# Groups of background products queued behind chosen products of the input GEMM, and GEMM products put between the pieces of the burst at the RWKV samples (one layer of an HGRN2 + RWKV-7 decoder)

## The chip, the cores and the metric

One core of one Trainium2 chip. The metric is the device time of one execution in microseconds (us), the median of several runs. The engines are TensorE (PE, with its weight loads PEld), VectorE (DVE), ScalarE (ACT), GpSimd (POOL) and SyncE (SP), which issues most transfers.

## What is computed

The reference is one inference step of one layer for a prompt of 512 tokens and 8 samples of 4 tokens, D_MODEL 1024, all in f32:

```python
h = RMSNorm(x)
u = h @ W_in          # 46 blocks of 128 columns: HGRN2 q,f,i,g | RWKV-7 r,k,v,lora | gates
# HGRN2 branch: 4 heads, state 128x128
S_t = diag(f_t) S_{t-1} + k_t v_t^T ;  o_t = S_t^T q_t
# RWKV-7 branch: 8 heads, state 64x64
S = S * w_t - (S kk_t)(kk_t a_t)^T + v_t k_t^T ;  y_t = S r_t
x = x + merge(sigmoid gates, projections of both branches)
x = x + relu(RMSNorm(x) @ W_up)^2 @ W_down
```

The outputs are y for prompt and samples, and both branches' new states.

## The kernel before

**The input GEMM.** Each block of 128 columns of W_in is one unit (`in_unit`, L411): its weights are loaded (`load8`, L175, 512 KB), split into a high and a low part (`split`, L167: ACT writes `whi`, DVE writes `wlo`), and `gemm_h` (L399) multiplies them with the normalised rows, kept as `h_hi` and `h_lo`. A unit is two halves of 272 columns, each 24 products: eight `h_hi,whi`, eight `h_hi,wlo`, eight `h_lo,whi`. All products pass through `mm` (L129). The results leave PSUM through ACT and DVE (`xq`, `xk`, `gt`, ...).

**The background.** The two branches run beside these GEMM products. The eight RWKV heads are four pairs p = 0 to 3 in two groups g = 0, 1. For a pair, `rw_batch` (L548) normalises k (`halves`, L534, splits the squares into `sxh` on ACT and `sxl` on POOL; `head_sums`, L540, sums them over a head on PE by two products with `sxh` and two with `sxl`; then a reciprocal `nrm` on DVE), makes `kkn`, `b`, `eb`, `kr`, sums `rk` in the same way into `bv`, and multiplies `kr` with `eb` (`rw_batch_pa`), which DVE masks into `A`. From `A`, by way of DRAM (`zb_d`), DVE inverts small blocks (`rw_inverse`, L669: `tmp`, `bn`, `xi`); then follow `rw_solve` and the chain over chunks. `rw_values` (L634) and `rw_tokens` (L647) make transposes and products with `VU`, `pav` and `BE`. `rw_sample` (L867) does the samples: for each pair 16 + 2 small products into `rw_sample_pz`, and then four rounds of eight small products, `rw_sample_pu`, each of which needs a DVE result (`rs` or `un`) made from the round before; the first round needs `rs` made from `pz` (`tsc(u0, zs, mneg, ...)`). `hg_head` (L1069) does an HGRN2 head: DVE and ACT make a decayed `X`, PE multiplies it (`hg_head_pu`, once for widths of 32 and once for 64), and its end transposes `hy` (`hg_head_pt`, L1160).

**What sets the order.** `ORDER` (L51) is a list by hand of units and of background stages; generators ("lanes") are advanced between units. What they emit is then put in order for each engine by a scheduler with its own estimates of durations; an engine executes its own instructions strictly in that order.

Of the kernel before, what the change touches and what calls it, by code (L numbers as in the profile page):

```python
# [61 lines left out]
def hybrid_step(ctx: ExitStack, tc: tile.TileContext, i, o):  # L62
# [1006 lines left out]
    def hg_head(L, h):  # L1069
# [34 lines left out]
        for hw, po_ in ((32, p32), (64, p64)):  # L1104
# [4 lines left out]
            for c in range(4):
                for u in range(64 // hw):  # L1110
                    s0 = 128 * c + 2 * hw * u
                    mm(po_[2 * hw * u:2 * hw * u + hw, c, :], X[:, s0:s0 + hw], X[:, s0 + hw:s0 + 2 * hw])
# [636 lines left out]
```

## Time and profile before

| | us |
|---|---|
| runs | 969.31, 972.62, 973.67; median 972.62 |
| profiled execution | 974.22 (span 972.5, mean granted clock 0.992) |
| PE busy | 933.1 (96% of the span) |
| DVE, ACT, POOL busy | 671.2, 444.4, 150.0 |

The profile is of one execution: start and duration of each instruction, and what an engine waited for when it was idle. A share of busy time over the whole span hides stages: the input GEMM with its background takes the part up to about 500 us, the MLP the rest. The change bears on the part from about 107 to 360 us. [...]

### The profile page before, as it was taken

The numbers are of one execution on the slowest core, as the hardware profiler recorded it, in microseconds if no ns is written. First come the engines' busy times: TensorE is split into PE (matmuls) and PEld (weight loads), VectorE is DVE, ScalarE is ACT, GpSimd is POOL, SyncE is SP. The second block draws the span as 40 slices with busy tenths as digits, with TensorE's granted clock in tenths as the row PEclk, the third lists the DMA queues.
The fourth block names the chain that finished last, engine by engine and source line by source line (L and its number), as shares of the span: only waits on it lengthen the run. The fifth ranks groups of instructions, "written<-read, shape, count | busy, mean of one in ns | idle before, by whom it ended". The sixth has DMA issues, their size and how long they took to land.

```text
span 972.5 us, 21434 instructions
## 1 busy us (share of the span) xinstructions
PE 933.1 (96%) x8756; PEld 880.5 (91%) x8756; DVE 671.2 (69%) x1362; ACT 444.4 (46%) x802; POOL 150.0 (15%) x340
## 2 busy tenths in 40 slices
PE   5999999899999899999999999999999999999995
PEld 5989987779899787888899999999999999999995
DVE  6634978769796864689878656675567667976433
ACT  7554546414636641344344334455444345435332
POOL 3487333222232101011000000000000000000000
PEclk9999999999999899999999999999999999999998
DMA  9633333312535142375734643246335533554111
GB/s 268 171 120 88 80 85 87 81 36 85 155 97 124 35 117 63 83 211 156 248 109 157 181 133 86 76 109 161 114 87 128 142 101 88 136 147 142 54 44 49
DMA packets 193204, 112.67 MB, mean 116 GB/s; under 512 B 39521, under 2 KB 179623, under 8 KB 193106
## 3 DMA queue, kind: packets, MB, share of 16 engines
q1 hardware_dynamic: 165808, 95.16, 33.7%
q10 hardware_dynamic: 25570, 9.85, 4.0%
q0 software_dynamic: 1728, 6.29, 3.4%
q8 instruction: 69, 1.13, 0.5%
q14 instruction: 29, 0.24, 0.1%
HBM read 85.08 MB, written 18.39 MB: 106 GB/s over the span
## 4 chain that ended last, share of the span: by engine, by line
PE 79%; DVE 10%; ACT 3%; DMA 3%; issue 2%; POOL 2%; SPq 0%; ACTq 0%; DVEq 0%; POOLq 0%
PE pd L130 25%; PE in_unit_ps L130 21%; PE full_unit_ps L130 17%; PE half_unit_ps L130 4%; PE rw_chain_pq L130 2%; PE rw_chain_py L130 1%; DVE tmp L136 1%; DVE wlo L136 1%; PE lora_ps L130 1%; PE rw_sample_pn L130 1%; PE hg_head_po L130 1%; PE rw_batch_pa L130 1%; DMA xin<-in_x_prompt_dram 1%; DVE X L136 1%; DMA zb_d<-A 1%
## 5 line engine op out<-in xcount | busy, mean ns | idle before, releaser
L133 ACT ACTIVATE whi<-st 128x1024 fp32r<-128x1024 f32 (+1 forms) x132 | 134.1, 1018 | 161.8 <-PE pd L130 65.6
L136 DVE TENSOR_TENSOR wlo<-st,whi 128x1024 fp32r<-128x1024 f32 (+1 forms) x120 | 142.6, 1190 | 34.1 <-ACT whi L133 11.2
L130 PE MATMUL in_unit_ps<-h_hi,whi 128*128 128x272 f32 (+3 forms) x736 | 119.6, 297 | 1.9 <-ACT h_hi L133 1.0
L130 PE MATMUL in_unit_ps<-h_hi,wlo 128*128 128x272 f32 (+3 forms) x736 | 119.6, 296 | 0.0
L130 PE MATMUL in_unit_ps<-h_lo,whi 128*128 128x272 f32 (+3 forms) x736 | 118.5, 295 | 0.0
L130 PEld LDWEIGHTS in_unit_ps<-h_hi,whi 128*128 128x128 f32 x736 | 101.6, 191 | 7.5 <-issue 3.4
L130 PE MATMUL full_unit_ps<-hd,whi 128*128 128x272 f32 (+2 forms) x736 | 108.3, 288 | 0.0
L130 PEld LDWEIGHTS in_unit_ps<-h_hi,wlo 128*128 128x128 f32 x736 | 101.7, 190 | 4.4 <-issue 2.3
L130 PEld LDWEIGHTS in_unit_ps<-h_lo,whi 128*128 128x128 f32 x736 | 101.2, 189 | 3.7 <-issue 1.9
L130 PEld LDWEIGHTS full_unit_ps<-hd,whi 128*128 128x128 f32 x736 | 98.6, 188 | 0.0
L130 PE MATMUL pd<-xgh,wlo 128*128 128x272 f32 x512 | 70.0, 288 | 0.0
L130 PE MATMUL pd<-xgl,whi 128*128 128x272 f32 x512 | 69.9, 288 | 0.0
L130 PE MATMUL pd<-xgh,whi 128*128 128x272 f32 x512 | 69.9, 288 | 0.0
L130 PEld LDWEIGHTS pd<-xgl,whi 128*128 128x128 f32 x512 | 66.5, 188 | 0.0
L130 PEld LDWEIGHTS pd<-xgh,wlo 128*128 128x128 f32 x512 | 66.5, 188 | 0.0
L130 PEld LDWEIGHTS pd<-xgh,whi 128*128 128x128 f32 x512 | 66.4, 188 | 0.0
L1602 POOL DMA_DIRECT2D slo<-st x12 | 10.5, 874 | 353.0 <-ACT slo L133 180.8
L136 DVE TENSOR_TENSOR x<-x,full_unit_ps 128x272 f32<-128x272 f32 (+3 forms) x40 | 20.8, 521 | 49.6 <-PE full_unit_ps L130 49.5
L130 PE MATMUL full_unit_ps<-hd,wlo 128*128 128x272 f32 (+2 forms) x272 | 47.7, 291 | 0.0
L130 PEld LDWEIGHTS full_unit_ps<-hd,wlo 128*128 128x128 f32 x272 | 38.8, 188 | 1.0
L133 ACT ACTIVATE gt<-in_unit_ps 128x272 f32<-128x272 f32 x32 | 12.6, 395 | 53.3 <-PE in_unit_ps L130 51.4
L139 DVE SCALAR_TENSOR_TENSOR r<-pd,rsb 128x272 f32<-128x272 f32 x64 | 25.1, 434 | 16.3 <-PE pd L130 14.3
(438 smaller groups left out, 1682.2 us busy)
## 6 DMA issues: line engine op xcount, KB each, us to landing
st<-in_w_in_dram SPq DMA_DIRECT2D x46, 512.0 KB
st<-in_w_up_dram SPq DMA_DIRECT2D x32, 512.0 KB
st<-in_w_down_dram SPq DMA_DIRECT2D x48, 256.0 KB
slo<-st POOLq DMA_DIRECT2D x12, 512.0 KB, 4.5
gt_d<-gt SPq DMA_DIRECT2D x16, 272.0 KB
st<-in_w_out_dram SPq DMA_DIRECT2D x8, 512.0 KB
st<-in_w_down_dram SPq DMA_DIRECT2D x8, 512.0 KB
gtb<-gt_d SPq DMA_DIRECT2D x8, 272.0 KB
```

The costliest lines, as they stand in the source:

```text
L130: T.matmul(out, lhsT, rhs, start=start, stop=stop)
L133: A.activation(out=out, in_=in_, func=func, **kw)
L136: (eng or V).tensor_tensor(out=out, in0=a, in1=b, op=op)
L139: V.scalar_tensor_tensor(out=out, in0=a, scalar=s, in1=b, op0=op0, op1=op1)
L1602: P.dma_start(out=w2.lo, in_=t2, accum_op=ALU.add)
```

## The change

`mm` returns its instruction; `gemm_h` counts each GEMM product in `gemms`. Inside `behind(n)`, every PE instruction that is issued gets an ordering dependency on GEMM product n: the scheduler may not place it earlier in PE's queue than that product. There is no semaphore, and no instruction of the arithmetic is added or removed. The constants give n for: the `sxl` products of `head_sums` of `bv` (PL_RK, per pair), the 32-wide `hg_head_pu` products of heads 0 and 1 (PL_PU), the `hy` transposes of head 1 (PL_HY), transposes of `eb` (PL_EB), the `pav` products of pairs 2, 3 (PL_AV), the `pz` products of pairs 1 to 3 (PL_PZ) and the first `pu` round (PL_SU).

```diff
+PL_RK = 612, 737, 1366, 1478
+PL_PU = {0: 946, 1: 1184}
+PL_HY = {1: 1280}
+PL_EB = {(0, 1): 848, (2, 0): 1560, (2, 1): 1560, (3, 0): 1568, (3, 1): 1568}
+PL_AV = {2: 1560, 3: 1568}
+PL_PZ = {1: 1576, 2: 1576, 3: 1584}
+PL_SU = {0: 1618}
...
     def mm(out, lhsT, rhs, start=True, stop=True):
-        T.matmul(out, lhsT, rhs, start=start, stop=stop)
+        return T.matmul(out, lhsT, rhs, start=start, stop=stop)
+    def queue(x, g):
+        tc.add_manual_dep(x, g.name, mybir.DependencyInfo(mybir.DependencyClass.NoSync, mybir.DependencyReason.DATA),
+                          reason="place")
+    @contextmanager
+    def behind(n):
+        cur = nc.cur_bb.bb.instructions
+        last = cur[-1]
+        yield
...
+        for x in cur[k + 1:]:
+            if x.engine == gemms[0].engine:
+                if n < len(gemms):
+                    queue(x, gemms[n])
+                else:
+                    places.setdefault(n, []).append(x)
...
-                    mm(ps, w[k], x[k][:, a:b], s == 0 and k == 0, s == 2 and k == K - 1)
+                    placed(mm(ps, w[k], x[k][:, a:b], s == 0 and k == 0, s == 2 and k == K - 1))
...
-    def head_sums(hi, lo):
+    def head_sums(hi, lo, n=None):
...
+            with behind(n) if k and n else nullcontext():
+                for j in range(2):
+                    mm(ps[:, j], bones, y[:, j * HALF:(j + 1) * HALF], k == 0, k == 1)
...
+            with behind(PL_SU[it]) if it in PL_SU else nullcontext():
```

The scheduler places everything else anew around these, so the queues of DVE, ACT, POOL and SP change too. Three places are shown (before first, the change second; line numbers of the two files differ).

The first: DVE's queue between `hy` of head 1 and the reciprocal of pair 2 (`nrm_3574`), with which the RWKV work of group 1 starts on DVE:

```order
L136 TENSOR_TENSOR hy_3472<-hy_3472,ss_h 128x512
L139 SCALAR_TENSOR_TENSOR hog_3499<-hg_head_pt_3494,prm,xq_2421 128x512
L142 TENSOR_SCALAR nrm_3574<-nrm_3574 128x544
L567 RECIPROCAL nrm_3574<-nrm_3574 128x544
L139 SCALAR_TENSOR_TENSOR xq_3663<-xq_3663,in_unit_ps_3613 128x272
L139 SCALAR_TENSOR_TENSOR kkn_3598<-xm_3229,prm,nrm_3574 128x544
```

```order
L172 TENSOR_TENSOR hy_3472<-hy_3472,ss_h 128x512
L175 SCALAR_TENSOR_TENSOR xq_3663<-xq_3663,in_unit_ps_3613 128x272
L175 SCALAR_TENSOR_TENSOR hog_3499<-hg_head_pt_3494,prm,xq_2421 128x512
L172 TENSOR_TENSOR wlo_3815<-st_3812,whi_3814 128x1024
L178 TENSOR_SCALAR nrm_3574<-nrm_3574 128x544
L604 RECIPROCAL nrm_3574<-nrm_3574 128x544
L175 SCALAR_TENSOR_TENSOR xq_3663<-xq_3663,in_unit_ps_3638 128x272
```

A GEMM result (`xq_3663`) and a weight split (`wlo_3815`) now stand ahead of the reciprocal. In POOL's queue a little later, the copy `ga<-xq_3758`, which stood behind pair 2's `sxl_3685`, now stands ahead of it.

The second: DVE's queue at the last mask of pair 3 (`A` from `rw_batch_pa_4018`), from which the inverse starts:

```order
L876 SCALAR_TENSOR_TENSOR rs_4138<-rst_351,gs 128x128
L136 TENSOR_TENSOR wlo_4545<-st_4542,whi_4544 128x1024
L136 TENSOR_TENSOR rs_4138<-rs_4138,gs 128x128
L136 TENSOR_TENSOR rs_4139<-gs,rs_4138 128x4x32
L136 TENSOR_TENSOR A_3989<-rw_batch_pa_4018,msk 128x256
L136 TENSOR_TENSOR A_3991<-rw_batch_pa_4018,msk 128x256
L136 TENSOR_TENSOR A_3990<-rw_batch_pa_4018,msk 128x256
L136 TENSOR_TENSOR A_3992<-rw_batch_pa_4018,msk 128x256
L136 TENSOR_TENSOR rs_4139<-gs,rs_4138 128x4x32 x3
```

```order
L915 SCALAR_TENSOR_TENSOR rs_4138<-rst_351,gs 128x128
L172 TENSOR_TENSOR rs_4138<-rs_4138,gs 128x128
L172 TENSOR_TENSOR rs_4139<-gs,rs_4138 128x4x32 x2
L172 TENSOR_TENSOR A_3989<-rw_batch_pa_4018,msk 128x256
L172 TENSOR_TENSOR A_3991<-rw_batch_pa_4018,msk 128x256
L172 TENSOR_TENSOR A_3990<-rw_batch_pa_4018,msk 128x256
L172 TENSOR_TENSOR A_3992<-rw_batch_pa_4018,msk 128x256
```

The four `A` now stand behind two `rs_4139<-gs,rs_4138`, the samples' keys times a decay from ACT, where before they stood behind one.

The third: the first rounds of the samples, on PE and on DVE. PE's queue at the first `pu` round; `in_unit_ps` are GEMM products, `rw_sample_pz` the end of the burst, `rw_sample_pu_4476` the first round and `rw_sample_pu_4492` the second:

```order
L130 MATMUL rw_sample_pz_4291<-s0T_4041,km_4365 64x64 x15
L130 MATMUL rw_sample_pz_4291<-rs_4141,rs_4140 64x64 x2
L130 MATMUL in_unit_ps_4548<-h_lo,whi_4544 128x272 x8
L130 MATMUL in_unit_ps_4573<-h_hi,whi_4544 128x272 x8
L130 MATMUL in_unit_ps_4573<-h_hi,wlo_4545 128x272 x8
L130 MATMUL in_unit_ps_4573<-h_lo,whi_4544 128x272 x8
L130 MATMUL in_unit_ps_4735<-h_hi,whi_4731 128x272 x4
L130 MATMUL rw_sample_pu_4476<-rs_4142,rs_4140 64x64 x8
L130 MATMUL in_unit_ps_4735<-h_hi,whi_4731 128x272 x4
L130 MATMUL in_unit_ps_4735<-h_hi,wlo_4732 128x272 x6
L130 MATMUL rw_sample_pu_4492<-rs_4142,rs_4140 64x64 x8
```

```order
L137 MATMUL rw_sample_pz_4291<-s0T_4041,km_4365 64x64 x16
L137 MATMUL rw_sample_pz_4291<-rs_4141,rs_4140 64x64 x2
L137 MATMUL in_unit_ps_4735<-h_hi,whi_4731 128x272 x7
L137 MATMUL in_unit_ps_4735<-h_hi,wlo_4732 128x272 x8
L137 MATMUL in_unit_ps_4735<-h_lo,whi_4731 128x272 x8
L137 MATMUL in_unit_ps_4760<-h_hi,whi_4731 128x272 x8
L137 MATMUL in_unit_ps_4760<-h_hi,wlo_4732 128x272 x3
L137 MATMUL rw_sample_pu_4476<-rs_4142,rs_4140 64x64 x8
L137 MATMUL in_unit_ps_4760<-h_hi,wlo_4732 128x272 x5
L137 MATMUL in_unit_ps_4760<-h_lo,whi_4731 128x272
L137 MATMUL rw_sample_pu_4492<-rs_4142,rs_4140 64x64 x8
```

The first round now stands 31 GEMM products further back: before, four of block 4735's first half lie ahead of it, now all 24 of that half (one of them ahead of the last `pz` piece) and 11 of the second half (4760). Between the first and the second round stood 10 products; now 6.

DVE's queue at the first `rs` of the samples (`rs_4142<-rs_4141`, what the first `pu` round waits for) and the second (`rs_4142<-rw_sample_pu_4476`, what the second round waits for):

```order
L136 TENSOR_TENSOR tmp_4060<-xi_4051,x_4052 128x512
L725 TENSOR_REDUCE bn_4050<-tmp_4060 128x32
L136 TENSOR_TENSOR tmp_4060<-bn_4050,x_4052 128x512
L142 TENSOR_SCALAR rs_4142<-rs_4141,mneg 128x256
L725 TENSOR_REDUCE bn_4050<-tmp_4060 128x8x8
L136 TENSOR_TENSOR tmp_4060<-bn_4050,x_4052 128x512
L139 SCALAR_TENSOR_TENSOR rs_4142<-rw_sample_pu_4476,mneg,rs_4142 128x256
L725 TENSOR_REDUCE bn_4050<-tmp_4060 128x4x8
```

```order
L175 SCALAR_TENSOR_TENSOR xq_4598<-xq_4598,in_unit_ps_4548 128x272
L172 TENSOR_TENSOR tmp_4060<-bn_4050,x_4052 128x512
L175 SCALAR_TENSOR_TENSOR xq_4598<-xq_4598,in_unit_ps_4573 128x272
L764 TENSOR_REDUCE bn_4050<-tmp_4060 128x8x8
L178 TENSOR_SCALAR rs_4142<-rs_4141,mneg 128x256
L172 TENSOR_TENSOR tmp_4060<-bn_4050,x_4052 128x512
L172 TENSOR_TENSOR s0T_4041<-s0T_4041,rs_4138 128x512
L764 TENSOR_REDUCE bn_4050<-tmp_4060 128x4x8
L172 TENSOR_TENSOR tmp_4060<-bn_4050,x_4052 128x512
L764 TENSOR_REDUCE bn_4050<-tmp_4060 128x4x8
L175 SCALAR_TENSOR_TENSOR rs_4142<-rw_sample_pu_4476,mneg,rs_4142 128x256
```

Two `xq` and one more `bn` stand ahead of the first `rs` now, and some rows earlier a seventh weight split (`wlo_4922`), where between `hy` and this `rs` stood six; one `s0T` (`s0T_4041`) has gone behind it. Between the first and the second `rs` stand two `tmp`, one `s0T` and two `bn`, where before stood one `tmp` and one `bn`.

## Rows read from the trace of the kernel before

**Rows 1.** The page, its first part: busy time, share of the span and instructions of each engine.

```profile
PE 933.1 (96%) x8756; PEld 880.5 (91%) x8756; DVE 671.2 (69%) x1362; ACT 444.4 (46%) x802; POOL 150.0 (15%) x340
```

**Rows 2.** The waits of PE from 100 to 345 us: who waits, for whom; us in total, times, the longest.

```profile
PE hg_head_pu L130 <- DVE X L136: 3.0, 1, 3.0
PE head_sums_ps L130 <- POOL sxl L136: 2.7, 4, 0.7
PE rw_sample_pu L130 <- DVE rs L142: 2.4, 1, 2.4
PE rw_batch_pt L662 <- ACT av L133: 1.6, 1, 1.6
PE hg_head_pt L1160 <- DVE hy L136: 1.4, 1, 1.4
```

**Rows 3.** Windows, busy us (and instructions) of PE, PEld, DVE, ACT, POOL, then the granted clock, the DMA share and GB/s.

```profile
160.00:180.00 20.00, 17.02 (x195) 15.33 (x194) 18.56 (x30) 8.95 (x16) 11.32 (x16) 1.00 0.46 125
...
200.00:240.00 40.00, 40.00 (x579) 33.91 (x578) 32.69 (x90) 11.34 (x20) 8.20 (x19) 1.00 0.23 70
...
260.00:280.00 20.00, 17.56 (x136) 16.77 (x135) 18.87 (x33) 10.41 (x15) 7.53 (x12) 1.00 0.45 122
...
320.00:340.00 20.00, 17.28 (x205) 15.55 (x205) 16.71 (x24) 11.54 (x18) 2.79 (x6) 0.83 0.19 40
```

**Rows 4.** The timeline of PE at the head sums of pairs 0 and 1, each with the idle time before it and its releaser in brackets.

```profile
109.01 0.52 PE L130 MATMUL head_sums_ps<-sxl,bones 128*128 128x272 f32 x2 [0.69 <-POOL sxl L136]
...
130.25 0.52 PE L130 MATMUL head_sums_ps<-sxl,bones 128*128 128x272 f32 x2 [0.73 <-POOL sxl L136]
```

**Rows 5.** The timeline of PE around the burst, from its first small products to the last `pu` round.

```profile
314.12 1.15 PE L130 MATMUL rw_sample_pz<-s0T,km 64*64 64x64 f32 x32
...
325.05 1.27 PE L130 MATMUL in_unit_ps<-h_lo,whi 128*128 128x272 f32 x8
...
329.16 0.67 PE L130 MATMUL in_unit_ps<-h_hi,whi 128*128 128x272 f32 x4
332.24 1.12 PE L130 MATMUL rw_sample_pu<-rs,rs 64*64 64x64 f32 x16 [2.41 <-DVE rs L142]
...
334.36 1.56 PE L130 MATMUL in_unit_ps<-h_hi,wlo 128*128 128x272 f32 x6
335.85 1.12 PE L130 MATMUL rw_sample_pu<-rs,rs 64*64 64x64 f32 x16
...
341.02 0.68 PE L130 MATMUL rw_sample_pu<-rs,rs 64*64 64x64 f32 x16
...
342.63 1.16 PE L130 MATMUL in_unit_ps<-h_lo,whi 128*128 128x272 f32 x8
343.63 1.17 PE L130 MATMUL in_unit_ps<-h_hi,whi 128*128 128x272 f32 x8
```

**Rows 6.** Windows of 2 us over the same stretch, columns as in group 3.

```profile
330.00:332.00 2.00, 0.00 (x0) 0.00 (x0) 1.93 (x4) 1.99 (x5) 0.37 (x2) 0.93 0.00 0
...
334.00:336.00 2.00, 2.00 (x11) 1.75 (x12) 2.00 (x4) 0.00 (x0) 0.00 (x0) 0.50 0.00 0
...
338.00:340.00 2.00, 2.00 (x26) 1.79 (x25) 0.44 (x2) 0.40 (x1) 0.46 (x2) 0.86 0.17 24
```

**Rows 7.** The timeline of DVE from `hy` of head 1 to `bv` of pair 2 and at pairs 2 and 3.

```profile
258.45 1.23 DVE L136 TENSOR_TENSOR wlo<-st,whi 128x1024 fp32r<-128x1024 f32 x1
...
262.74 0.69 DVE L136 TENSOR_TENSOR hy<-hy,ss_h 128x512 f32<-128x512 f32 x1
...
265.32 3.55 DVE L567 RECIPROCAL nrm<-nrm 128x544 f32<-128x544 f32 x1
268.79 0.38 DVE L139 SCALAR_TENSOR_TENSOR xq<-xq,in_unit_ps 128x272 f32<-128x272 f32 x1
...
277.25 2.37 DVE L136 TENSOR_TENSOR wlo<-st,whi 128x1024 fp32r<-128x1024 f32 x1
...
304.01 1.42 DVE L136 TENSOR_TENSOR A<-rw_batch_pa,msk 128x256 f32<-128x256 f32 x4
307.09 0.69 DVE L136 TENSOR_TENSOR rs<-gs,rs 128x128 f32<-128x128 f32 x3 [1.66 <-ACT rs L133]
```

**Rows 8.** The timeline of POOL in the same stretch.

```profile
258.63 2.28 POOL L136 TENSOR_TENSOR sxl<-sq,sxh 128x544 fp32r<-128x544 f32 x1 [3.19 <-ACT sxh L133]
...
277.05 1.49 POOL L136 TENSOR_TENSOR sxl<-rk,sxh 128x544 fp32r<-128x544 f32 x1 [2.41 <-ACT sxh L133]
278.48 1.21 POOL L1039 COPY ga<-xq 128x32 f32<-128x32 f32 x1
```

**Rows 9.** The timeline of DVE in the inverse of group 1, up to the `rs` of the first and the second `pu` round.

```profile
320.58 1.22 DVE L136 TENSOR_TENSOR wlo<-st,whi 128x1024 fp32r<-128x1024 f32 x1
...
327.49 0.69 DVE L136 TENSOR_TENSOR s0T<-s0T,rs 128x512 f32<-128x512 f32 x1
...
331.84 0.34 DVE L142 TENSOR_SCALAR rs<-rs,mneg 128x256 f32<-128x256 f32 x1
332.11 0.68 DVE L725 TENSOR_REDUCE bn<-tmp 128x64 f32<-128x512 f32 x1
332.81 1.03 DVE L136 TENSOR_TENSOR tmp<-bn,x 128x512 f32<-128x512 f32 x1
333.76 0.47 DVE L139 SCALAR_TENSOR_TENSOR rs<-rw_sample_pu,mneg,rs 128x256 f32<-128x256 f32 x1
```

More of the change, by code (lines that the diff above doesn't have):

```diff
@@ L1 @@
-from contextlib import ExitStack
+from contextlib import ExitStack, contextmanager, nullcontext
 import concourse.bass as bass
@@ L129, in mm, with placed @@
     def mm(out, lhsT, rhs, start=True, stop=True):
-        T.matmul(out, lhsT, rhs, start=start, stop=stop)
+        return T.matmul(out, lhsT, rhs, start=start, stop=stop)
+    gemms, places = [], {}
+    def queue(x, g):
[6 more added lines that the diff above has]
+        yield
+        cur = nc.cur_bb.bb.instructions
+        k = len(cur) - 1
+        while cur[k] is not last:
+            k -= 1
+        for x in cur[k + 1:]:
[4 more added lines that the diff above has]
+                    places.setdefault(n, []).append(x)
+    def placed(ins):
+        for x in places.pop(len(gemms), ()):
+            queue(x, ins.ins)
+        gemms.append(ins.ins)
     def act(out, in_, func=AF.Copy, **kw):
@@ L538, in halves @@
         return hi, lo
-    def head_sums(hi, lo):
+    def head_sums(hi, lo, n=None):
         ps = pe("head_sums_ps")[:, :, 0:HALF]
         for k, y in enumerate((hi, lo)):
-            for j in range(2):
-                mm(ps[:, j], bones, y[:, j * HALF:(j + 1) * HALF], k == 0, k == 1)
+            with behind(n) if k and n else nullcontext():
+                for j in range(2):
+                    mm(ps[:, j], bones, y[:, j * HALF:(j + 1) * HALF], k == 0, k == 1)
         return ps
@@ L650, in rw_tokens @@
         g, e = p // 2, p % 2
-        for n in range(8):
-            for h in range(2):
+        with behind(PL_AV[p]) if p in PL_AV else nullcontext():
+            for n in range(8):
+              for h in range(2):
                 mm(pav[64 * h:64 * h + 64, n, :], Az[p, h][0:64, n, :], VU[g, n // 2][0:64, n % 2, e, h, :])
@@ L660, in rw_tokens @@
             pt = LX.one("rw_batch_pt")
-            for n in range(4):
-                T.transpose(pt[:, 128 * n:128 * n + 128], chan[p][j][:, n].rearrange("p m w -> p (m w)"), ident)
+            with behind(PL_EB[p, j]) if (p, j) in PL_EB else nullcontext():
+                for n in range(4):
+                    T.transpose(pt[:, 128 * n:128 * n + 128], chan[p][j][:, n].rearrange("p m w -> p (m w)"), ident)
             BE[p, j] = S(512, name="BE").rearrange("p (n h w) -> p n h w", n=4, h=2)
@@ L914, in rw_sample @@
                           in_=kr[:, p].rearrange("p m (b t) -> p b m t", t=NT))
-            for b in range(NB):
+            with behind(PL_PZ[p]) if p in PL_PZ else nullcontext():
+              for b in range(NB):
                 for h in range(2):
@@ L927, in rw_sample @@
             pu = L.one("rw_sample_pu")[:, 0:256].rearrange("p (q w) -> p q w", q=4)
-            for p in range(4):
-                for h in range(2):
-                    mm(pu[64 * h:64 * h + 64, p, :], ms[64 * h:64 * h + 64, p, :], u[64 * h:64 * h + 64, p, :])
+            with behind(PL_SU[it]) if it in PL_SU else nullcontext():
+                for p in range(4):
+                    for h in range(2):
+                        mm(pu[64 * h:64 * h + 64, p, :], ms[64 * h:64 * h + 64, p, :], u[64 * h:64 * h + 64, p, :])
             if it < 3:
@@ L1108, in hg_head @@
             yield
[L1109 to L1112, printed above, removed]
+            with behind(PL_PU[h]) if hw == 32 and h in PL_PU else nullcontext():
+                for c in range(4):
+                    for u in range(64 // hw):
+                        s0 = 128 * c + 2 * hw * u
+                        mm(po_[2 * hw * u:2 * hw * u + hw, c, :], X[:, s0:s0 + hw], X[:, s0 + hw:s0 + 2 * hw])
         for u in range(2):
@@ L1158, in hg_head @@
         pt = L.one("hg_head_pt")
-        for c in range(4):
-            T.transpose(pt[:, 128 * c:128 * c + 128], y[:, c, :], ident)
+        with behind(PL_HY[h]) if h in PL_HY else nullcontext():
+            for c in range(4):
+                T.transpose(pt[:, 128 * c:128 * c + 128], y[:, c, :], ident)
         og = L.S(512, name="hog")
```

2 lines of the change are left out of this document (1 added, 1 removed).

## The prediction

> **What bounds the kernel now.** I read the page first: PE is busy for 96% of the span [rows 1], so what an order can gain is idle PE time and time at half clock. The waits of PE in the touched part come next [rows 2]: 3.0 us at `hg_head_pu` for DVE's `X`, 2.7 at four head sums for POOL's `sxl`, 2.4 at the first sample round for DVE's `rs`, 1.6 at a transpose behind `av`, 1.4 at the `hy` transposes. They sum to 11.1 us. Each of the change's pins sits at one of them. Then the windows [rows 3] say who owns each stretch. In 200 to 240 us PE is busy all 40 of 40 us: there PE owns the time. In 160 to 180 DVE is busy 18.56 of 20, in 260 to 280 18.87, against PE's 17.02 and 17.56: there PE waits for DVE. Last, the timeline at the burst [rows 5]: small products begin at 314.12, GEMM products are back from 325.05, the last four begin at 329.16, and then PE stands idle 2.41 us until the first `pu` round at 332.24. [...]
>
> The reader should see that PE's idle time before the first round is not a hole in PE's order alone. DVE is in the inverse of group 1, back to back, and `rs` comes at 331.84 [rows 9]. Whoever fills the 2.41 us with GEMM products gains only as long as `rs` does not come later too.
>
> **The change, part by part.** Nothing is computed more or less; only queues change. A 272-column product costs 0.125 us at full clock (eight between 342.63 and 343.63) and 0.25 at half (six between 334.36 and 335.85) [rows 5].
>
> Up to 265 us: the pins on pairs 0 and 1 remove 0.69 and 0.73 us [rows 4], those on `hg_head_pu`, `eb` and `hy` 3.0, 1.6 and 1.4 [rows 2], 7.4 together. As an upper end this is kept whole; the lower end is nothing. I count nothing at the end, because PE is not what the first sample round waits for: time that PE wins ahead of it lengthens its wait, unless more products can be done there. That is counted below.
>
> The chain to the first round, on DVE. By how much is `rs` later than 331.84?
> - The reciprocal of pair 2 now has one `xq` and one weight split ahead of it: 0.38 + 1.23 = 1.6 us [rows 7]. If the `xq` lies in a wait it is 1.2; I take 1.6.
> - On POOL the copy `ga` (1.21) stands ahead of pair 2's `sxl` [rows 8]. Before, POOL was idle ahead of `sxl`, so part of it is covered: I take 0.8, between 0 and 1.2.
> - The masks `A` of pair 3 stand behind an `rs_4139` that needs ACT's decay. DVE waited 1.66 us for this at 307.09, after the `A` at 304.01 [rows 7]. Now the `A` wait with it: 1.66 and the 0.23 of one product of three in 0.69, 1.9 in all. The lower end is 0, if ACT is earlier by as much; the upper is 3.1, from 304.01 to 307.09.
> - Ahead of `rs` stand a seventh `wlo`, two more `xq` and one more `bn`, and one `s0T` fewer: 1.22 + 2 x 0.38 + 0.68 - 0.69 = 2.0 us [rows 7, 9]. DVE has no hole there, so this is whole.
>
> Together 6.3 us, between 3.2 (the first at 1.2, the second and third at 0) and 7.9.
>
> PE's part. The first round stands 31 GEMM products further back: 31 x 0.125 = 3.9 us of work that is done before it now and not after. A round that comes 6.3 us later with 3.9 us more behind it leaves +2.4 us.
>
> The second round waits for the `rs` that DVE makes from the first. Between the two `rs` stood `bn` 0.68 and `tmp` 1.03; now two of each and an `s0T` 0.69 [rows 9]: 4.1 us and not 1.7, so 2.4 more. Between the rounds stand six products, not ten: 0.5 us less to cover with. Together +2.9; the lower end is 0, if PE comes so late that `rs` is there.
>
> The clock. The 6.8 us at half clock cost at most 3.4. Part of that is lost in the third round's wait for DVE anyway, so I take 2.5 back: the burst has GEMM products between its pieces, and the wait ahead of the first round is shorter. The lower end is no gain at all, if the new wait behind the first round lowers the clock in its turn.
>
> Sum: 0 + 2.4 + 2.9 - 2.5 = +2.8 us. By its ends: 3.2 - 3.9 + 0 - 3.4 = -4.1, and 7.9 - 3.9 + 2.9 - 0 = +6.9. The profiled execution took 974.2, so 977.0; it stands 1.6 above the median of the runs, so I forecast 975.4 us, and by the ends 968.5 to 979.5.
>
> One thing is a choice of order between DVE and POOL. At 277.05 `sxl` began first and took 1.49, and the `wlo` begun at 277.25 took 2.37 and not 1.2; at 258.45 a `wlo` began first and took 1.23, and the `sxl` begun at 258.63 took 2.28 [rows 7, 8]. [...] By the rows that is 2.28 - 1.49 = 0.8 us on this chain, where before it was DVE's split that paid. I leave it out of the sum, since I cannot tell which starts first; with it the forecast would be 976.2.
>
> **The rivals.**
> - Faster: the chain on DVE is not delayed. For it speaks that PE saves up to 7.4 us ahead of 265 and owns 200 to 240 [rows 3], so that group 1 could start earlier by what its queue loses. Then the 31 products fill the wait: -3.9, and the clock gives back 2.5: 974.2 - 6.4 - 1.6 = 966.2 us. Against it: four separate delays stand in DVE's and POOL's queues, and DVE has little room (18.87 of 20 busy).
> - Slower: the wait ahead of the second round, with few products between the rounds, takes the place of the one removed, and the clock falls to half behind it as it did behind the 2.41 us. Its place is PE between the first and the fourth `pu` round. Then the 2.5 is not won, and with the blocked `sxl` the sum is 2.4 + 0.8 + 2.9 = +6.1: 978.7 us. It decides from the point where `rs` is over 6 us later than before and the clock at 0.50 for as long as before. Against it: the 3.0 us of idle time at `hg_head_pu` had the clock at 1.00 [rows 2, 3].
> - No effect: a pin only holds a product back, and the planner's times are not the chip's. If `sxl` is later by as much as the products that now stand ahead of it, the waits come back at the same places, and the 31 products and the later `rs` cancel: 3.9 of delay, no clock gain, 972.6 us.
>
> **How the numbers follow.** A measurement of this kernel tells about 0.5% from no change, 4.9 us: faster is below 967.7, slower above 977.5. My forecast, a delayed chain with the clock kept, has 0.42; it lies within the bound, with a tail over it of 0.04 inside that chance. The slower rival has 0.27, the faster 0.16, no effect 0.15. Same is 0.38 + 0.15 = 0.53, slower 0.27 + 0.04 = 0.31, faster 0.16. The range, 966 to 980 us, goes from the faster rival to the upper end of the sum, and leaves out the faster rival's better half and both effects of the slower one at their upper ends; the forecast's own is 972 to 979.5.
>
> **What would show it.** Right: the 3.0 us before `hg_head_pu` of head 0 and the 1.4 before the `hy` transposes are gone; the reciprocal of pair 2 begins about 2 us later than 265.32; `A` of pair 3 ends 4 us or more later; the first `rs` of the samples comes about 338 and not 331.84; PE waits over 1 us ahead of the second round; the clock stays at 1.00 there. Wrong: the first `rs` at 334 or earlier, and PE without a wait at the first two rounds (the faster rival), or the clock at 0.50 for 5 us or more after 335 (the slower one). That the reciprocal of pair 2 begins no later would break the first step.

## The result and the profile after

| kernel | runs | median us | lowest to highest |
|---|---|---|---|
| before | 20 | 973.38 | 968.82 to 976.74 |
| changed | 20 | 978.53 | 973.84 to 982.72 |

The ratio is 1.0061, with a 95% interval of 1.0045 to 1.0077: the change costs 0.6%, 4.4 to 7.5 us. The profiled execution of the changed kernel took 973.84 us, with a span of 972.1 and a mean granted clock of 0.989. It is the fastest of its 20 runs, as fast as the profiled execution of before, so the two totals show no difference. What the profile tells is where the waits now are. One of the 12 runs of c_first below, of 982.80 us, was slow, and all figures leave it out.

The page, first part, which answers to [rows 1]:

```profile
PE 932.0 (96%) x8756; PEld 879.3 (90%) x8756; DVE 669.2 (69%) x1362; ACT 442.6 (46%) x801; POOL 147.9 (15%) x340
```

The waits of PE from 100 to 345 us, which answer to [rows 2] (us in total, times, the longest):

```profile
PE head_sums_ps L137 <- POOL sxl L172: 3.3, 3, 1.7
PE rw_sample_pu L137 <- DVE rs L175: 2.6, 1, 2.6
PE head_sums_ps L137 <- ACT sxh L169: 2.0, 3, 0.8
PE rw_batch_pt L679 <- DVE A L172: 1.6, 2, 1.2
PE rw_batch_pav L137 <- ACT BE L169: 1.2, 1, 1.2
PE rw_out_pt L137 <- DVE yo L172: 1.0, 1, 1.0
```

The 3.0 at `hg_head_pu`, the 1.6 behind `av` and the 1.4 at the `hy` transposes are gone. In their places stand waits that before had not among its first five: ACT's `sxh` at the head sums, the mask `A`, `BE`, `yo`. These six sum to 11.7 us, the five of before to 11.1.

The timeline of PE at the four `pu` rounds, which answers to [rows 5]:

```profile
334.76 0.68 PE L137 MATMUL rw_sample_pu<-rs,rs 64*64 64x64 f32 x16
338.97 0.68 PE L137 MATMUL rw_sample_pu<-rs,rs 64*64 64x64 f32 x16 [2.57 <-DVE rs L175]
341.70 1.12 PE L137 MATMUL rw_sample_pu<-un,rs 64*64 64x64 f32 x16
343.93 0.68 PE L137 MATMUL rw_sample_pu<-rs,rs 64*64 64x64 f32 x16
```

The first round now runs without a wait; the second waits 2.57 us, where the first had waited 2.41. The rows of DVE on the way there, which answer to [rows 7, 9]:

```profile
261.76 0.69 DVE L172 TENSOR_TENSOR hy<-hy,ss_h 128x512 f32<-128x512 f32 x1
...
264.50 1.23 DVE L172 TENSOR_TENSOR wlo<-st,whi 128x1024 fp32r<-128x1024 f32 x1
266.12 3.55 DVE L604 RECIPROCAL nrm<-nrm 128x544 f32<-128x544 f32 x1
...
277.77 1.21 DVE L172 TENSOR_TENSOR wlo<-st,whi 128x1024 fp32r<-128x1024 f32 x1
280.95 0.72 DVE L172 TENSOR_TENSOR bv<-head_sums_ps,xm 128x544 f32<-128x544 f32 x1 [1.96 <-PE head_sums_ps L137]
...
307.37 0.56 DVE L172 TENSOR_TENSOR rs<-gs,rs 128x128 f32<-128x128 f32 x2 [1.82 <-ACT rs L169]
307.85 1.41 DVE L172 TENSOR_TENSOR A<-rw_batch_pa,msk 128x256 f32<-128x256 f32 x4
...
311.00 1.22 DVE L172 TENSOR_TENSOR wlo<-st,whi 128x1024 fp32r<-128x1024 f32 x1
314.68 0.18 DVE L724 COPY xi<-bn 128x8 f32<-128x8 f32 x1 [2.46 <-DMA bn<-zb_d]
...
334.17 0.34 DVE L178 TENSOR_SCALAR rs<-rs,mneg 128x256 f32<-128x256 f32 x1
...
338.34 0.48 DVE L175 SCALAR_TENSOR_TENSOR rs<-rw_sample_pu,mneg,rs 128x256 f32<-128x256 f32 x1
```

The reciprocal of pair 2 begins 0.80 later, the masks `A` 3.84 later (304.01 before), but the first `rs` only 2.33 later (331.84 before). POOL, which answers to [rows 8]:

```profile
277.56 1.50 POOL L1080 COPY ga<-xq 128x32 f32<-128x32 f32 x1 [2.66 <-DVE xq L175]
279.02 1.32 POOL L172 TENSOR_TENSOR sxl<-rk,sxh 128x544 fp32r<-128x544 f32 x1
```

The copy goes first, takes 1.50 beside DVE's `wlo` of 277.77, and `sxl` begins 1.97 later than the 277.05 of before. DVE has to wait 1.96 ahead of `bv` for it, by way of the head sums.

Windows (columns as in group 3 of the rows of before; the granted clock is the number behind POOL's):

```profile
14.00:24.00 10.00, 9.27 (x48) 7.55 (x46) 9.07 (x35) 8.21 (x21) 7.24 (x8) 0.66 1.13 297
154.00:160.00 6.00, 5.98 (x59) 5.91 (x60) 5.24 (x6) 3.77 (x6) 1.47 (x2) 0.72 0.56 123
...
338.00:344.00 6.00, 5.03 (x49) 4.47 (x51) 2.83 (x5) 1.34 (x2) 0.00 (x0) 0.72 0.61 130
```

Half clock, a granted clock of 0.50, follows the new wait as it followed the old one, for 0.28 x 6 / 0.5 = 3.4 us and not 6.8. But it also stands at 14 to 24, ahead of everything that the change moved, and at 154 to 160, where one execution of the order before (h_before, below) has it too.

**Two parts of a run's time.** Each run reports its mean granted clock, so its time can be split. (1 - clock) x time is what it lost to half clock, if a stretch at 0.50 loses half of its length. The rest, clock x time, is then what it would have taken at full clock throughout. Over the 94 runs of before beside the experiments, the loss is 7.6 ± 0.5 us and the rest 965.0 ± 0.4 (means). Over 26 of the changed kernel (the 20, and 6 of the next section) it is 10.9 ± 1.0 and 968.5 ± 0.9. So by this split **about +3.5 us are work and waits of the order and about +3.3 are time at half clock**. (The clocks of the 20 runs of before in the first table are not on record.) Experiments are read by both numbers. All ± are 1.96 standard errors; with 6 to 12 runs that is a little narrow for 95%.

The split counts every microsecond at half clock as half lost, 0.97 us of time for each 0.001 of mean clock, and the runs show less: 0.51 ± 0.12 among the 94 runs of before, 0.80 ± 0.33 among the 26 of the changed kernel, 0.64 within all kernels together. Why is not shown; probably part of the half-clock time lies in waits that are there anyway. At 0.64 the changed kernel is +4.6 ± 0.9 at the same clock, and only about 2 us go with the clock. So the two parts are known to a microsecond or two, and differences of that size between orders are read with this in mind.

### The profile page after: what moved, and what is told of

It reads as the page before. It is cut to its first block, busy times and chain, and to the rows that moved or that the text cites. A ratio compares the mean times of both kernels' runs of the same rounds, so it can differ in the third digit from the quotient of the medians.

```text
span 972.1 us, 21438 instructions
## 1 busy us (share of the span) xinstructions
PE 932.0 (96%) x8756; PEld 879.3 (90%) x8756; DVE 669.2 (69%) x1362; ACT 442.6 (46%) x801; POOL 147.9 (15%) x340
## 4 chain that ended last, share of the span: by engine, by line
PE 70%; DVE 14%; DMA 5%; ACT 4%; issue 3%; POOL 2%; SPq 0%; ACTq 0%; DVEq 0%; POOLq 0%
PE pd L137 22%; PE full_unit_ps L137 17%; PE in_unit_ps L137 17%; PE half_unit_ps L137 4%; DVE tmp L172 2%; PE rw_chain_pq L137 2%; DMA st<-in_w_down_dram 2%; DVE wlo L172 1%; PE rw_chain_py L137 1%; DVE nrm L604 1%; DVE bn L764 1%; PE rw_sample_pn L137 1%; PE lora_ps L137 1%; DMA bn<-zb_d 1%; ACT whi L169 1%
## 5 line engine op out<-in xcount | busy, mean ns | idle before, releaser
L172 DVE TENSOR_TENSOR wlo<-st,whi 128x1024 fp32r<-128x1024 f32 (+1 forms) x120 | 141.3, 1178 | 35.2 <-ACT whi L169 11.1
```

Of the source, the lines that this page charges most:

```text
L172: (eng or V).tensor_tensor(out=out, in0=a, in1=b, op=op)
```

## The experiments

The first theory was the prediction's (the chain theory of the expectations): a delayed chain on DVE makes `rs` late, and the wait moves to the second round. The rivals: the wait at the second round alone costs the time, whatever the chain does (wait theory); the first half of the program (up to 265 us) costs it; or nothing in the order does, and the clock alone differs (clock theory).

All results together. The last column is the idle time of PE from `hy` of head 1 to the first `rw_solve_py` behind the rounds, summed over the brackets of PE's timeline in the one profile of each kernel.

| kernel | runs | median us | ratio to before, 95% | half-clock loss | rest | PE idle |
|---|---|---|---|---|---|---|
| before | 94 | 972.4 | | 7.6 ± 0.5 | 965.0 ± 0.4 | 5.8 |
| changed (again) | 6 | 980.8 | 1.0097, 1.0060 to 1.0133 | 12.3 ± 2.9 | 969.4 ± 1.7 | 9.4 (first profile 7.6) |
| b_rs | 12 | 973.3 | 1.0023, 0.9997 to 1.0048 | 10.0 ± 2.3 | 964.9 ± 0.9 | 6.1 |
| a_rs2 | 11 | 978.6 | 1.0070, 1.0043 to 1.0097 | 10.0 ± 2.3 | 968.5 ± 1.1 | 7.7 |
| a_undo | 9 | 976.6 | 1.0052, 1.0030 to 1.0073 | 9.8 ± 2.2 | 967.6 ± 1.2 | 7.1 |
| c_first | 11 | 974.2 | 1.0015, 0.9989 to 1.0041 | 9.0 ± 1.8 | 965.2 ± 1.3 | 6.6 |
| c_second | 12 | 974.7 | 1.0027, 1.0010 to 1.0044 | 7.1 ± 1.4 | 968.0 ± 0.8 | 8.3 |
| c_burst | 12 | 974.4 | 1.0018, 1.0002 to 1.0035 | 8.8 ± 1.2 | 965.4 ± 1.2 | 6.3 |
| h_before | 12 | 971.7 | 0.9997, 0.9983 to 1.0012 | 6.9 ± 0.9 | 965.0 ± 0.6 | 5.8 |
| c_mid | 12 | 974.7 | 1.0026, 1.0006 to 1.0047 | 9.3 ± 0.9 | 965.6 ± 1.2 | 7.1 |
| r_before | 12 | 973.6 | 1.0001, 0.9983 to 1.0018 | 7.5 ± 1.7 | 965.7 ± 1.1 | 6.1 |
| r_after | 12 | 976.5 | 1.0043, 1.0018 to 1.0067 | 9.5 ± 2.4 | 967.3 ± 1.6 | 6.0 |
| a_pu2 | 11 | 979.1 | 1.0062, 1.0035 to 1.0089 | 10.9 ± 2.6 | 968.7 ± 1.2 | 8.8 |

Except for `again`, each kernel is the kernel before with a table `HOLD`, which lists every engine's instructions in the wanted order. At the end of `hybrid_step`, ordering dependencies without a semaphore hold that order:

```diff
+    byname = {x.name: x for x in nc.cur_bb.bb.instructions}
+    for nums in HOLD.values():
+        seq = [byname[f"I-{n}"] for n in nums.split()]
+        for a, b in zip(seq, seq[1:]):
+            tc.add_manual_dep(b, a.name, mybir.DependencyInfo(mybir.DependencyClass.NoSync,
+                                                              mybir.DependencyReason.DATA), reason="hold")
```

So only the table differs between them, and in r_before and r_after the reciprocals as well. The diffs below show the rows of the order that it moves.

**The changed kernel again.** No edit.

> The changed kernel once more, unchanged, for a second profile and for the granted clock of each run. Chain theory (the loss is DVE's work of group 1, which is later, so that PE waits ahead of the second sample round): median 977 to 980 us, about 5 above before, and a profile in which PE's idle time from 100 to 360 us is at least as large as before's 15 us, whatever the clock. [...]

Its profile, DVE and then PE at the same places (the second round):

```profile
314.03 1.41 DVE L172 TENSOR_TENSOR A<-rw_batch_pa,msk 128x256 f32<-128x256 f32 x4
323.07 0.18 DVE L724 COPY xi<-bn 128x8 f32<-128x8 f32 x1 [4.67 <-DMA bn<-zb_d]
...
342.53 0.34 DVE L178 TENSOR_SCALAR rs<-rs,mneg 128x256 f32<-128x256 f32 x1
```

```profile
347.33 1.12 PE L137 MATMUL rw_sample_pu<-rs,rs 64*64 64x64 f32 x16 [2.78 <-DVE rs L175]
```

This run's start was longer: its first `nrm` reciprocal begins at 99.83, against 94.98 in the first profile, and 4.85 has to be taken off all times to compare. Then `A` comes 1.3 us later than in the first profile, the first `rs` 3.5 later, 6.1 later than before. The round trip of `zb` through DRAM makes most of that: from the start of `A` to the `xi` it feeds went 6.8 us in the first profile and 9.0 here. The second round waits in both. The median, 980.8, lies just above the chain theory's 977 to 980. The clock theory wants more time at half clock than before; between 100 and 520 us it is not there: three stretches of 3.4 us, 10 in all, where before has 6.8 and 3.4.

**b_rs: the old order, with the first `rs` made early on DVE.** PE's order stays.

```diff
 TENSOR_SCALAR xk_4442<-xk_4442,lbt 128x544
+TENSOR_SCALAR rs_4142<-rs_4141,mneg 128x256
 TENSOR_TENSOR tmp_4060<-xi_4051,x_4052 128x512
 TENSOR_REDUCE bn_4050<-tmp_4060 128x32
+SCALAR_TENSOR_TENSOR rs_4142<-rw_sample_pu_4476,mneg,rs_4142 128x256
 TENSOR_TENSOR tmp_4060<-bn_4050,x_4052 128x512
-TENSOR_SCALAR rs_4142<-rs_4141,mneg 128x256
...
-SCALAR_TENSOR_TENSOR rs_4142<-rw_sample_pu_4476,mneg,rs_4142 128x256
```

The later `un`, `rs` and `xq` move up in the same way.

> The kernel before with every engine's order held, except that on DVE the rs that the first sample round waits for stands four rows earlier (ahead of three rows of the inverse), and the rs, un and xq behind it likewise. Clock theory: the 2.4 us of idle time ahead of the first round and the 6.8 us at half clock behind it go, 4 to 5 us faster than before (968 to 970). Chain theory: the inverse of group 1 is later by the rows that now stand ahead of it (about 1.7 us), PE waits for its result near 350 us, and 1 to 2 us are won at most (972 to 974).

```profile
329.72 0.68 PE L544 MATMUL rw_sample_pu<-rs,rs 64*64 64x64 f32 x16
331.78 0.68 PE L544 MATMUL rw_sample_pu<-rs,rs 64*64 64x64 f32 x16
...
335.77 0.68 PE L544 MATMUL rw_sample_pu<-rs,rs 64*64 64x64 f32 x16
345.07 0.31 PE L544 MATMUL rw_solve_py<-XT,zb 32*32 32x32 f32 x2 [2.49 <-DVE rs L550]
```

All four rounds run without a wait, 5 us earlier at the last, and the 2.4 us come back at `rw_solve_py`: DVE did the rounds' rows ahead of the inverse's, so the inverse is later. The rest is unchanged (964.9), and the clock theory's 968 to 970 did not come. The 2.41 us of the kernel before were not to be won by moving DVE's rows.

**a_rs2 and a_undo: the new order, with rows of DVE put back.** a_rs2 moves the `rs` that the second round waits for ahead of the inverse's rows; a_undo also moves the four `A` ahead of both `rs_4139` and `wlo_3815` back behind pair 2's reciprocal.

```diff
 TENSOR_SCALAR rs_4142<-rs_4141,mneg 128x256
 TENSOR_TENSOR tmp_4060<-bn_4050,x_4052 128x512
+SCALAR_TENSOR_TENSOR rs_4142<-rw_sample_pu_4476,mneg,rs_4142 128x256
 TENSOR_TENSOR s0T_4041<-s0T_4041,rs_4138 128x512
 TENSOR_REDUCE bn_4050<-tmp_4060 128x4x8
 TENSOR_TENSOR tmp_4060<-bn_4050,x_4052 128x512
 TENSOR_REDUCE bn_4050<-tmp_4060 128x4x8
-SCALAR_TENSOR_TENSOR rs_4142<-rw_sample_pu_4476,mneg,rs_4142 128x256
```

> The changed kernel with every engine's order held, except that on DVE the rs made from the first sample round stands four rows earlier. Both theories expect the 2.6 us wait ahead of the second round to go. Chain theory: the inverse is later by 0.5 us, so 0 to 2 us faster than the changed kernel. Clock theory: the half-clock time behind that wait (3.4 us in the profile) goes too, so 3 to 4 us faster than the changed kernel, about 975.

> The changed kernel with every engine's order held, except for three undone moves on DVE: the rs made from the first round stands four rows earlier, the four masks A of pair 3 stand ahead of the product that waits for ACT's decay, and the weight split stands behind the reciprocal of pair 2. Chain theory: the inverse starts 2 to 3 us earlier, and the kernel is 3 to 5 us faster than the changed one, 973 to 975. Clock theory: as with the first of the three moves alone (975), within 1 us.

PE in a_rs2, the second and the third round:

```profile
338.11 0.68 PE L544 MATMUL rw_sample_pu<-rs,rs 64*64 64x64 f32 x16
342.34 0.68 PE L544 MATMUL rw_sample_pu<-un,rs 64*64 64x64 f32 x16 [2.23 <-DVE un L553]
```

The wait went one round on, and the rest stayed at 968.5; the median, 978.6, is not the clock theory's 975. With the masks and the split put back too, 0.9 ± 1.5 us came back (967.6); the median, 976.6, misses what both theories expected (973 to 975, and 975 within 1). The rows of DVE that the prediction priced do not carry the 3.5 us one by one.

**c_first, c_second, c_burst: the change in parts.** c_first has the changed order up to 262.5 us and the old one behind it; c_second the old one up to 263.4 us and the changed one behind it; c_burst the old one up to 313.9 us, where the burst begins, and the changed one from there. The edit is the table: at the cut the rest of each engine's row of numbers is taken from the other kernel.

> Every engine's order held: the changed kernel's order up to 262 us (just ahead of the hy transposes of head 1), the order before from there. Chain theory: PE loses the 3.0 us of idle time at head 0's hg_head_pu and the like, but waits for the same rs at the first sample round, so 972 to 974, within 1 us of before. Idle theory (each us of PE idle time removed is won): 2 to 3 us less idle time from 150 to 200 us, 969.5 to 971.

> Every engine's order held: the order before up to 263 us, the changed kernel's from there (head sums of pairs 2 and 3, masks, burst, sample rounds). Chain theory: this half carries the whole loss, masks A of pair 3 some 4 us later, 977 to 980. Clock theory: no later than the changed kernel's share of half-clock time makes it, 973 to 976, and runs sorted by their clock.

> Every engine's order held: the order before up to 314 us, the changed kernel's from there, so only the burst of small products with GEMM products put between and the sample rounds. Chain theory: the masks A of pair 3 are as early as before; rs is later by the 2.0 us of rows moved ahead of it, the 31 products cover 3.9, the second round waits about 2.5: 972 to 975, within 2 us of before. If the loss of the change lies in the burst, 976 to 979.

The rest: +0.2 ± 1.3 with the first part alone, +3.0 ± 0.9 with the second alone, +0.4 ± 1.3 with the burst alone; at the same clock by the slope of 0.64, +0.7 ± 1.5, +2.9 ± 0.8 and +0.8 ± 1.1. So most of the order's cost lies behind 263 us, and not in the burst's own order. But c_second's median, 974.7, misses the chain theory's 977 to 980: of the change's whole difference (+0.6 to 1.0%) it carries 0.27%, since its runs lost no more to half clock than before's. c_first's 974.2 speaks against the idle theory (969.5 to 971); c_burst's 974.4 is as the chain theory expected. Why the first part wins nothing, though the 3.0 at `hg_head_pu` is gone, its waits of PE from 100 to 360 us show:

```profile
PE rw_sample_pu L544 <- DVE rs L556: 2.4, 1, 2.4
...
PE rw_batch_pav L544 <- ACT BE L547: 1.8, 1, 1.8
PE head_sums_ps L544 <- ACT nrm L547: 1.5, 1, 1.5
...
PE in_unit_ps L544 <- DVE xq L553: 1.0, 1, 1.0
```

`BE`, `nrm` and `xq` were not waited for so long before: PE comes earlier to each next step that another engine has to finish. PE in c_burst:

```profile
316.61 1.92 PE L1056 MATMUL rw_batch_pt<-ident,xm 128*64 128x128 f32 x8 [2.75 <-ACT VU L547]
338.14 0.68 PE L544 MATMUL rw_sample_pu<-rs,rs 64*64 64x64 f32 x16
340.24 0.68 PE L544 MATMUL rw_sample_pu<-rs,rs 64*64 64x64 f32 x16 [0.47 <-DVE rs L553]
```

With the burst's products in the new order but the stretch ahead of it as before, the first round waits for nothing and the second 0.47 us. A wait of 2.75 for `VU` has appeared at the burst's beginning, and the 2.41 has gone in exchange.

**h_before and c_mid.** h_before holds the order before unchanged, and so prices the table itself. c_mid has the changed order only in the middle: before up to 263.4 us, changed up to the first `pz` product (314.9), before again behind it.

> The kernel before with its own order held on every engine: the same instructions in the same order, for the granted clock of each run and a second profile of the order before. Both theories: the same as before, 971 to 975. Clock theory: the mean granted clock of its runs is 0.991 or more, against 0.989 in the changed kernel's 20 runs. Chain theory: the clocks do not differ by more than 0.001.

> Every engine's order held: the order before up to 263 us, the changed kernel's from there up to the first small product of the burst, and the order before again from the burst on. For each run the time is split into what half clock cost (1 minus the mean granted clock, times the time) and the rest; before: rest 965.1, changed: 968.5, second half alone 968.0, burst alone 965.4. Chain theory: the masks of pair 3 are some 3 us later as in the second half, so the rest is 967 to 968.5 without any change in the burst or the rounds. If the loss needs the new order of the sample rounds as well, the rest is 965 to 966.

h_before is the kernel before (0.9983 to 1.0012). Its windows at 154 to 160 and at the burst, the latter against the clock of [rows 6]:

```profile
154.00:160.00 6.00, 4.45 (x50) 3.95 (x49) 5.22 (x7) 3.17 (x8) 1.52 (x2) 0.79 0.46 95
...
330.00:340.00 10.00, 7.59 (x100) 6.64 (x99) 9.90 (x16) 4.43 (x7) 1.51 (x4) 1.00 0.06 7
```

The order is the same, PE waits 2.4 us for `rs` here too, and the clock stays at 1.00. r_before, with the same order and a wait of 2.42, also has 1.00 there. That half clock followed the old wait was so in one execution and not in two others. The mean clock of h_before's runs is 0.993 against 0.989 of the changed kernel, as the clock theory expected; the chain theory's limit of 0.001 did not hold.

c_mid's rest is +0.6 ± 1.3, where the theory that the middle carries the cost had 967 to 968.5: this fell. PE in c_mid and then in c_second:

```profile
325.93 1.12 PE L1076 MATMUL rw_batch_pt<-ident,eb 128*128 128x128 f32 x4 [2.18 <-ACT BE L547]
336.24 0.68 PE L544 MATMUL rw_sample_pu<-rs,rs 64*64 64x64 f32 x16
338.29 0.68 PE L544 MATMUL rw_sample_pu<-rs,rs 64*64 64x64 f32 x16
```

```profile
335.68 0.68 PE L544 MATMUL rw_sample_pu<-rs,rs 64*64 64x64 f32 x16 [0.40 <-DVE rs L556]
340.08 0.68 PE L544 MATMUL rw_sample_pu<-rs,rs 64*64 64x64 f32 x16 [2.76 <-DVE rs L553]
```

In c_mid the middle's delay is taken up ahead of the rounds (2.18 for `BE`), where before PE would have waited for `rs`, and the old rows of DVE let the second round go on at once. In c_second the first round has its 31 products, but the second has six products ahead of it and five rows of DVE, and waits 2.76. Middle and burst alone add 0.6 and 0.4; together 3.0. The surplus, 2.0, has an uncertainty of about 2, and at the same clock by the slope of 0.64 it shrinks to 0.9 (1.2 and 0.8 against 2.9). That the cost takes both is how the waits read, and it is not shown.

**r_before and r_after: is the chain bound by DVE's load?** In both orders, the reciprocals of pairs 2 and 3 (3.55 us each) are cut to one column; k of these pairs is then not normalised, only clamped.

```diff
-            tsc(nrm[p], nrm[p], 1e-12, ALU.max)
-            V.reciprocal(out=nrm[p], in_=nrm[p])
+            tsc(nrm[p], nrm[p], 1e-12, ALU.max, *((0.05, ALU.min) if p >= 2 else ()))
+            if p < 2:
+                V.reciprocal(out=nrm[p], in_=nrm[p])
+            else:
+                V.reciprocal(out=warm, in_=nrm[p][:, 0:1])
```

> The order before, held on every engine, with DVE relieved: the reciprocals of pairs 2 and 3 (3.5 us each) are made on one column only and the norm is capped at 0.05 in its place, so k of these pairs is not normalised. Chain theory: DVE's chain of group 1 is up to 7 us shorter, PE's waits from 265 to 335 us shrink and the rest falls by 2 to 4 us, to 961 to 963. If DVE is not what this stretch waits for, the rest stays at 965.

> The changed kernel's order, held, with the same relief of DVE (reciprocals of pairs 2 and 3 on one column, k of these pairs not normalised). Chain theory: the loss of the change was DVE's lateness, so most of it goes: the rest is within 1 us of the relieved kernel before, against 3.4 us apart without relief. If the loss lies in PE's own order, the two stay 3 us apart.

DVE in r_before:

```profile
266.14 0.16 DVE L984 RECIPROCAL warm<-nrm 128x1 f32<-128x1 f32 x1
268.13 0.44 DVE L553 SCALAR_TENSOR_TENSOR xq<-xq,in_unit_ps 128x272 f32<-128x272 f32 x1 [1.83 <-ACT xq L547]
...
279.80 0.72 DVE L550 TENSOR_TENSOR bv<-head_sums_ps,xm 128x544 f32<-128x544 f32 x1 [1.80 <-PE head_sums_ps L544]
...
282.39 1.42 DVE L550 TENSOR_TENSOR A<-rw_batch_pa,msk 128x256 f32<-128x256 f32 x4 [1.80 <-PE rw_batch_pa L544]
```

About seven microseconds of DVE's work were taken out of the stretch that I called DVE's, and the rest stayed at 965.7 ± 1.1 against 965.0: DVE waits 1.8 us each for ACT, for the head sums and for PE instead. Its queue stands between GEMM results and small products of PE, in a fixed order, and its 94% in the window (18.87 of 20 us in [rows 3]) did not mean that its work set the pace. r_after, at 967.3 ± 1.6, lies between the two orders and decides nothing.

**a_pu2: the new order with more products ahead of the second, third and fourth round**, each 18 GEMM products further back (the expectation has 20 for the third).

```diff
 MATMUL rw_sample_pu_4476<-rs_4142,rs_4140 64x64 x8
 MATMUL in_unit_ps_4760<-h_hi,wlo_4732 128x272 x5
-MATMUL in_unit_ps_4760<-h_lo,whi_4731 128x272
+MATMUL in_unit_ps_4760<-h_lo,whi_4731 128x272 x8
+MATMUL in_unit_ps_4925<-h_hi,whi_4921 128x272 x8
+MATMUL in_unit_ps_4925<-h_hi,wlo_4922 128x272 x3
 MATMUL rw_sample_pu_4492<-rs_4142,rs_4140 64x64 x8
```

> The changed kernel's order, held, except that on PE the second, third and fourth sample rounds stand 18, 20 and 18 GEMM products later, so that 24 products and not 6 lie between the first and the second. Wait theory (the 2.6 us ahead of the second round are lost because PE has too little to do there): the wait goes and the rest is 2 to 3 us lower than the changed kernel's 968.5, 965.5 to 966.5. Chain theory in its strict form (the end of this stretch is set by DVE wherever PE stands): the wait moves to a later place and the rest falls by less than 1 us.

```profile
341.75 0.68 PE L544 MATMUL rw_sample_pu<-rs,rs 64*64 64x64 f32 x16 [0.55 <-DVE rs L553]
...
348.83 0.24 PE L544 MATMUL rw_solve_py<-XT,zb 32*32 32x32 f32 x2 [1.71 <-DVE XT L1152]
```

The wait ahead of the second round shrank to 0.55, but the rest stayed at 968.7: 1.71 appeared at `rw_solve_py`, and smaller ones ahead of it. So the wait at the second round alone does not cost the time; the theory that it does expected 965.5 to 966.5. None of these orders is faster than the one before.

## Why the prediction came out as it did

The time, 978.5, lies in the range (966 to 980), and 5.1 above the median beside it. I forecast +2.8, within what a measurement can tell; it is slower by 0.61%, a little beyond it. That it came so close is in part luck: the sum had +5.3 for work and waits and -2.5 for the clock, and by the split +3.5 and +3.3 were measured, two errors of opposite sign. The steps:

- **Nothing won ahead of 265 us: right as far as can be told.** DVE's `hy` began 0.98 us earlier (261.76, 262.74 before), but in c_first nothing of it is left in the whole kernel (rest +0.2 ± 1.3).
- **The reciprocal 1.6 later, the copy 0.8, the masks 1.9 more: the sizes partly wrong, the sum for the masks right.** From DVE's `hy` to the reciprocal went 2.58 us before and 4.36 after, 1.8 more, so the two rows were paid in full; the reciprocal came only 0.80 later because `hy` was earlier. The copy delayed `sxl` by more than I took: from `rk` to `sxl` went 1.54 us before and 2.64 after, so 1.1. `A` begins 4.1 and 5.4 us later in the two profiles, counted from the first `nrm`; 4.3 was the sum.
- **`rs` 6.3 later: 2.6 in one profile and 6.1 in the other, counted from the first `nrm`.** Two things were wrong. The sum missed the round trip of `zb` through DRAM between `A` and the inverse: from `A` to `xi` it took 8.8 us before, 6.8 and 9.0 after, so it gave back 2.0 in one execution and nothing in the other. And "DVE has no hole there" does not hold. DVE waited for that round trip before, too:

```profile
312.83 0.17 DVE L685 COPY xi<-bn 128x8 f32<-128x8 f32 x1 [1.83 <-DMA bn<-zb_d]
```

The split at 311.00 now runs in this wait, and from `xi` to `rs` went 19.0 us before and 19.5 in both profiles of the change: +0.5 where the sum had 2.0. So 4.1 - 2.0 + 0.5 = 2.6, and 5.4 + 0.2 + 0.5 = 6.1. The forecast "about 338" for the first `rs` failed at 334.17, just above the 334 at which the faster rival would have held.
- **A wait of over 1 us ahead of the second round: right,** 2.57 and 2.78; I had 2.9. But read as a price at this place it is wrong: in a_rs2 and a_pu2 the wait is moved or shortened there, and the rest does not fall. What the order costs goes along with PE's idle time over the whole stretch from `hy` to `rw_solve_py`; that this idle time is the cost is likely and not shown. The four orders with the new middle and the new burst together, and the changed kernel, have 7.1 to 9.4 us of it and a rest of +2.6 to +3.7; the kernels with one of them or none 5.8 to 6.6 and -0.1 to +0.7. c_mid (7.1, +0.6) and r_after (6.0, +2.3) fit less well; the idle time is that of one execution each, and in the changed kernel's first profile it is 1.8 us more than before, not 3.5.
- **The clock, -2.5: wrong, and in its sign.** This is the step that failed. No run shows the 2.5: the loss to half clock rose from 7.6 to 10.9 us on average, +3.3 by the split and about 2 by the slope of 0.64. The 6.8 us that the 2.5 was taken from are a reading of [rows 6] and of the two windows between those rows, 0.07 x 2 / 0.5 + 6.0 + 0.14 x 2 / 0.5:

```profile
332.00:334.00 2.00, 1.76 (x19) 1.64 (x20) 1.97 (x4) 1.02 (x2) 0.00 (x0) 0.50 0.00 0
...
336.00:338.00 2.00, 2.00 (x21) 1.88 (x22) 1.12 (x3) 0.00 (x0) 0.00 (x0) 0.50 0.00 0
```

I had taken them, because they stand behind the old wait, as a price of that wait; h_before has the same wait at full clock, and the changed kernel's profile has half clock at 338 to 344 behind the new wait, for 3.4 us, and at 14 to 24, which the change does not touch.
- **The blocked `sxl`, left out of the sum: POOL paid, in another place.** The 0.8 was the difference of two `sxl` of before, 2.28 and 1.49; that it would fall on pair 2's was my estimate. In the changed kernel that `sxl` began at 279.02, behind the `wlo` (277.77 + 1.21 = 278.98), and took 1.32. But the copy ahead of it overlapped that whole split and took 1.50 us. In c_second, with the same order on both engines, the copy took 0.36 and the `sxl`, begun inside the split of 278.21 to 279.43, took 2.27:

```profile
278.00 0.36 POOL L1453 COPY ga<-xq 128x32 f32<-128x32 f32 x1 [2.65 <-DVE xq L553]
278.36 2.27 POOL L550 TENSOR_TENSOR sxl<-rk,sxh 128x544 fp32r<-128x544 f32 x1
```

From the start of `rk` to the end of `sxl` went 3.0 us before, 4.0 in the changed kernel and 3.8 in c_second, so the copy and the overlap with the split together cost 0.8 to 0.9 here. Which of the overlapping instructions took longer does not follow here from their starts in the profile: in c_second the split began first and the `sxl` was the long one (2.27), but in the changed kernel the copy began 0.21 us ahead of the split and took 1.50 all the same.
- **The slower rival** had the right signs, a wait at the second round and half clock behind it, and at 978.7 the right time, but not the right way to it: it wanted `rs` over 6 us late and the clock low there for as long as before.

What stays open: which part of the change raises the time at half clock. By parts it is +1.4 ± 1.9 (c_first), -0.5 ± 1.5 (c_second), +1.2 ± 1.3 (c_burst) and +1.7 ± 1.0 (c_mid); these do not tell one part from another. One place speaks for the first part. Of the seven profiles with the changed order up to 262 us, five have 3.4 us at half clock that begin between 154.9 and 156.6; of the seven with the old order there, only h_before has such a stretch, from 157.5. PE waits 1.1 to 1.8 us for ACT just ahead of this place in all fourteen. With one execution each that is a hint, worth about 1 of the 3.3 us. Other half-clock time lies behind the part that the change moves: 3.4 to 6.8 us between 475 and 491 in seven of the fourteen profiles, of either order. Nor is it shown why c_mid, with 1.3 us more idle time, has hardly a longer rest.

## What to carry over

In a stretch in which two engines hand results to each other in fixed order, neither's busy share need say who sets the pace (here 7 us less work on a DVE that was 94% busy left the rest at 965.7, against 965.0), and a wait taken away at one place can come back at the next handover (here the 2.4 at `rs` as 2.49 at `rw_solve_py`): sum the idle time of the bounding engine over the whole stretch, before and after, and do not price one wait. Before a stretch at half clock is put down to the wait ahead of it, look at a second execution of the same order. Where the total of one profile and the median of many runs differ by as much as the effect, split each run by its mean clock, and see from the runs how much of a microsecond at half clock reaches the total: here about two thirds of what the split takes.

## What the runs showed of the hardware that was not expected

- The time of a run goes with its mean granted clock, loosely: among the changed kernel's 20 runs those at 0.986 took 979.2 to 982.7 us, those at 0.992 took 975.7 to 977.1, but the four at 0.989 took 973.8 to 981.4.
- The stretches at half clock stand at other places in other executions: 330 to 340 in one of the order before and not in two others (h_before, r_before), 14 to 24, 154 to 160 and 338 to 344 in one of the changed kernel.
- The same program's start, up to the first `nrm` reciprocal, took 94.98 us in one execution and 99.83 in another.
- The way of `zb` out to DRAM and back into `bn`, measured from the start of `A` to the `xi` copy, took 6.8 us in one execution and 9.0 in another of the same kernel, and 8.8 in one of before.
- A POOL copy that began 0.21 us ahead of a VectorE split of 1.21 took 1.50 us in two executions of the changed kernel, and 0.36 in c_second and c_mid, where it began as far ahead; the split itself took 1.21 in the first profile of the changed kernel and 1.22 in c_second.
